# A chunked state recurrence with a shorter way back, two more kinds of copies and sums on the vector engine, and weight splits that no longer alternate between two engines

## The chip, the cores and the metric

The kernel runs on one core of one Trainium2 chip. The metric is device time in microseconds (us) of one execution. The engines are named as the profile names them: PE is the matrix engine, PEld its weight loads, DVE the vector engine, ACT the scalar engine, POOL the general engine (GpSimd), SP the engine that issues most DMAs.

## The reference

A network of two blocks over 256 context and 256 latent tokens. The change touches one layer of it, an S5 mixer: 128 groups of 16 channels, each with 64 complex states and two directions, that run over time by a linear recurrence in chunks. Cut to what matters for the change:

```python
def s5_scan(u, abar, bbar, cmat, h0):
...
        bu = jnp.einsum('btgn,gpn->btgp', u_blk.astype(jnp.complex64), bbar)
        bu = bu.at[:, 0].add(abar[None] * h)
...
        _, hs = lax.associative_scan(_linrec_combine, (a, bu), axis=1)
        y = jnp.einsum('btgp,gnp->btgn', hs, cmat).real
...
# s5_mixer, for each direction: the context first, then the latents from its last state
        yc_dir, h_ctx = s5_scan(flip_seq(uc, rev), abar, bbar, cmat, h0)
        y_dir, _ = s5_scan(flip_seq(u, rev), abar, bbar, cmat, h_ctx)
        y = y + flip_seq(y_dir, rev)
...
        g = jax.nn.gelu(t.reshape(bsz, n, E_WIDTH))
        return (g * jax.nn.sigmoid(g @ w + bias)).astype(p.dtype)
```

In words: each state is the decay times the state before plus an input term, s_t = a s_(t-1) + B u_t. The kernel needs y for the latents only; from the context it needs the last state.

## The kernel before, in words

The mixer runs over 512 tokens cut into 64 chunks of 8 steps (32 of the context and 32 of the latents). It works in four quarters q0 to q3 of 32 groups. For each quarter there are stages, each a Python generator in `s5_mix`:

- u: the input product for 512 channels in four units of weights (PE lines L200 to L202), then four evacuations from PSUM (the accumulator memory) by ACT into tiles of the ring Q.
- t: PE transposes of these tiles (L998), evacuated by ACT (L149, `h<-pm`, 128x512).
- x: eight passes of chunk sums (PE L1017), each evacuated by ACT into `Sc` (context) and `S` (latents); after the eighth, `recur` does the recurrence on DVE and makes `hy`, eight copies of S for PE.
- y: what the states give and what the inputs give in the same chunk (PE L1100 and L1077), then a gelu on ACT and DVE. y needs `hy` of its own quarter.
- z: the gate's product in four units, each evacuated by ACT as a tanh and a copy into one Q tile; the gate is then formed from both halves.
- g: the product of gelu and gate, which is the input of the GLU.

The stages are traced in one hand-written order:

```python
STAGES = "u0 z0/1 t0 z0/1 x0 u1 z0/1 t1 z0/1 x1 u2 z1/1 t2 y0 x2 w0 z1/1 u3 t3 y1 x3 w1 z1/2 z2 y2 w2 z3 y3 g0 g1 g2 w3 g3"
```

(z0/1 is one of the four units of z0; w is the last step of a y.) A scheduler then orders the instructions of each engine; every engine runs its own list in order. Tiles are taken from rings: a new tile of a ring takes the place of the one that was allocated so many tiles before, and its first writer waits until that one's last reader is done. The ring Q (`qslot`, 128x512) has 9 places and serves u, z, gelu and the temporaries `t1`, `t2` of `recur`; staged weights `st` have 6 places, split weights `wl` 3, PSUM tiles `pm` 4 and `pa` 3. The small temporaries `rt` of the serial part of `recur` have two places of their own.

Every weight unit (`wunit`) is loaded by SP into `st`, copied by ACT into its rounded half (`hi`, L149 `wl<-st` 128x1024), and the remainder (`lo = st - hi`, L152 `wl<-st,wl`) is formed by DVE or POOL as the pattern `lo_pat` says, letter by letter ("V" is DVE, "P" is POOL).

`recur` works in two parts. The first goes up over the 32 context chunks: five levels of sums, each of two products and two sums (a complex multiplication by a power of the decay from `ap`, a table loaded for each quarter), 24 instructions of up to 128x512 elements. The second goes through the 32 latent chunks one after the other: 31 times two products and two sums of 128x64.

Of the kernel before, what the change touches and what calls it, by code (L numbers as in the profile page):

```python
# [5 lines left out]
F32 = mybir.dt.float32  # L6
# [3 lines left out]
AF = mybir.ActivationFunctionType  # L10
ALU = mybir.AluOpType
# [94 lines left out]
def bc(ap, *dims):  # L106

    return bass.AP(tensor=ap.tensor, offset=ap.offset, ap=[list(ap.ap[0])] + [list(d) for d in dims])


class Builder:
# [850 lines left out]
    def s5_mix(self, hT, W):  # L962

        nc = self.nc
# [38 lines left out]
        def x_quarter(q):  # L1003
            ut = uts[q]
            Sc = self.S5.tile([128, 2, 32, 32], F32, tag="Sc", name="Sc", bufs=1)
            S = self.S5.tile([128, 2, 33, 32], F32, tag="S", name="S", bufs=2)
            for i in range(8):
                w = self.ST.tile([128, 1024], F32, tag="st", name="st")[:, :].rearrange("p (o x) -> p o x", o=4)
                self.dma(w, self.wd[:, 32 * q:32 * q + 32, :, :].rearrange("p (o i) d x -> p i o (d x)", i=8)[:, i])
                ps = self.pms()  # L1010
                for o in range(4):
                    g = 8 * o + i
                    x = ut[g // 16][:, g % 16, :]
                    xb = bass.AP(tensor=x.tensor, offset=x.offset + 31, ap=[list(x.ap[0]), [32, 2], [-1, 32]])
                    for r in range(2):
                        for d in range(2):
                            nc.tensor.matmul(ps[64 * d:64 * d + 64, r * 256 + o * 64:r * 256 + (o + 1) * 64],  # L1017
                                             w[:, o, d * 128 + r * 64:d * 128 + r * 64 + 64],
                                             x if d == 0 else xb, start=True, stop=True, tile_position=(0, 64 * d))
                pv = ps[:, :].rearrange("p (r o c) -> p r o c", r=2, o=4)  # L1020
                self.copy_a(Sc[:, :, :, i::8].rearrange("p r c o -> p r o c"), pv[:, :, :, :32])
                self.copy_a(S[:, :, 1:, i::8].rearrange("p r c o -> p r o c"), pv[:, :, :, 32:])
                if i == 7:
                    recur(q, Sc, S)
                yield

        def recur(q, Sc, S):
            ap = self.S5.tile([128, 5, 3, 32], F32, tag="ap", name="ap")
            self.dma(ap[:, :, :, :].rearrange("p a b g -> p (a b) g"),
                     self.apd[:, :, :, 32 * q:32 * q + 32].rearrange("p a b g -> p (a b) g"))  # L1030

            for k in range(5):
                st = 2 << k
                n = min(16 >> k, 8)
                for s0 in range((1 << k) - 1, 32, st * n):
                    t1, t2 = (self.qslot()[:, :64 * n].rearrange("p (r c g) -> p r c g", r=2, c=n) for _ in range(2))
                    x = bc(Sc[:, 0, s0, 0:1], (1024, 2), (32 * st, n), (1, 32))
                    xs = Sc[:, 1, s0, 0:1]
                    xs = bass.AP(tensor=xs.tensor, offset=xs.offset, ap=[list(xs.ap[0]), [-1024, 2], [32 * st, n], [1, 32]])
                    z = bc(Sc[:, 0, s0 + (1 << k), 0:1], (1024, 2), (32 * st, n), (1, 32))  # L1040
                    self.mul(t1, x, bc(ap[:, k, 0, 0:1], (0, 2), (0, n), (1, 32)))
                    self.mul(t2, xs, bc(ap[:, k, 1, 0:1], (32, 2), (0, n), (1, 32)))
                    self.add(t1, t1, z)
                    self.add(bc(S[:, 0, 0, 0:1], (1056, 2), (32, 1), (1, 32)) if k == 4 else z, t1, t2)
            are, aim = bc(ap[:, 0, 0, :], (0, 2), (1, 32)), ap[:, 0, 1:3, :]
            for c in range(1, 32):
                t = self.S5.tile([128, 2, 2, 32], F32, tag="rt", name="rt", bufs=2)
                old = S[:, :, c - 1, :]
                sw = bass.AP(tensor=old.tensor, offset=old.offset + 1056, ap=[list(old.ap[0]), [-1056, 2], [1, 32]])
                self.mul(t[:, 0], old, are)  # L1050
                self.mul(t[:, 1], sw, aim)
                self.add(S[:, :, c, :], S[:, :, c, :], t[:, 0])
                self.add(S[:, :, c, :], S[:, :, c, :], t[:, 1])
            hy = hys[q]
            hy += [self.S5.tile([128, 2, 16, 32], F32, tag="hy", name="hy", bufs=4) for _ in range(2)]
            for a in range(2):
                for r in range(2):
                    sc = 1.0 if r == 0 else -1.0
                    f = S[0:64, r, 0:32, a * 16:(a + 1) * 16].rearrange("p c g -> p g c")
                    b = S[64:128, r, 31, a * 16:a * 16 + 1]  # L1060
                    b = bass.AP(tensor=b.tensor, offset=b.offset, ap=[list(b.ap[0]), [1, 16], [-32, 32]])
                    nc.scalar.activation(hy[a][0:64, r, :, :], f, AF.Copy, scale=sc)
                    nc.scalar.activation(hy[a][64:128, r, :, :], b, AF.Copy, scale=sc)

        def y_quarter(q):
            ut, hy = uts[q], hys[q]
# [57 lines left out]
        def z_quarter(q):  # L1124
            if q < 2:
                zt = self.hslot()
            elif q == 2:
                zs.append(self.S5.tile([128, 2048], F32, tag="Sc", name="zs"))
            zt = (zt if q < 2 else zs[0][:, 1024 * (q - 2):1024 * (q - 1)])[:, :].rearrange("p (o x) -> p o x", o=4)
            for o in range(4):  # L1130
                ps = self.pacc()
                w = self.w_ws(W, 2048 + q * 512 + o * 128)
                for kt in range(8):
                    xs = [hT[kt][:, r, :].rearrange("p (s c) -> p s c", s=8)[:, :, 32:] for r in range(2)]
                    self.mm3(ps[:, :256].rearrange("p (s c) -> p s c", s=8), w[kt], xs, kt == 0, kt == 7)
                th = self.qslot()
                nc.scalar.activation(th[:, :256], ps[:, :256], AF.Tanh, scale=0.5)
                self.copy_a(th[:, 256:], ps[:, :256])
                self.mul(zt[:, o, :], th[:, :256], th[:, 256:], nc.gpsimd)
                self.add(zt[:, o, :], zt[:, o, :], th[:, 256:], nc.gpsimd)  # L1140
                if o == 3:
                    Z[q] = zt
                yield
# [19 lines left out]
        for stage in STAGES.split():  # L1163
            gs = []
            for p in stage.split("+"):
                p, _, n = p.partition("/")
                name = p.replace("w", "y")
                if name not in open_:
                    f, steps = gen[name[0]]
                    open_[name] = f(int(name[1])), steps  # L1170
                g, steps = open_[name]
# [807 lines left out]
    def build(self):  # L1979
        tc = self.tc  # L1980
        with tc.tile_pool(name="C", bufs=1) as self.C, \
                tc.tile_pool(name="H", bufs=16) as self.H, \
                tc.tile_pool(name="Q", bufs=9) as self.Q, \
                tc.tile_pool(name="T", bufs=8) as self.T, \
                tc.tile_pool(name="ST", bufs=NST) as self.ST, \
                tc.tile_pool(name="WL", bufs=NHI) as self.WL, \
                tc.tile_pool(name="DR", bufs=1, space=DRAM) as self.DR, \
                tc.tile_pool(name="PA", bufs=NPA, space=PSUM) as self.PA, \
                tc.tile_pool(name="PM", bufs=NPM, space=PSUM) as self.PM, \
                tc.tile_pool(name="PF", bufs=1, space=PSUM) as self.PF:  # L1990
            self.setup()
            with tc.tile_pool(name="SB", bufs=1) as self.SB, tc.tile_pool(name="E", bufs=NE) as self.E:
                self.extra = NE
                self.block1_l0()
                if "x1n" in self.dbg:
                    for b in range(4):
                        self.dma(self.dbg["x1n"][b * 128:(b + 1) * 128, :], self.x1[b])
                self.block2_vectors()
            self.lo_pat = "VP"
            self.off = tc.nc.gpsimd  # L2000
            self.extra = 0
            with tc.tile_pool(name="S5", bufs=1) as self.S5:
                G = self.block1_l1()
            with tc.tile_pool(name="X", bufs=1) as self.X, tc.tile_pool(name="E2", bufs=12) as self.E:
                self.extra = 8
                self.block2(self.block1_glu(G))
# [27 lines left out]
```

## Time and profile before

| | |
|---|---|
| median of 3 runs | 2326.35 us (2323.8 to 2330.18) |
| profiled execution, its own time | 2329.09 us |
| span in the profile | 2327.2 us (1.89 us lie outside it) |
| granted TensorE clock, mean | 0.909 of full |
| PE / DVE busy | 2030.9 us (87%) / 1429.4 us (61%) |
| ACT / POOL busy | 875.5 us (38%) / 749.3 us (32%) |
| DMA, mean | 158 GB/s |

PE is the engine that is busy most. The S5 layer lies between about 690 and 1130 us of the span. A busy share over the whole span says little of the stage that the change touches; for that one reads the windows, the waits and the timelines of that stretch.

### The profile page before, as it was taken

The page shows a single profiled execution, that of the slowest core. Times are in us where ns is not written, and L with a number is a line of the kernel's source. Part 1 is how long each engine was busy: PE and PEld are TensorE (multiplying, and loading weights), DVE is VectorE, ACT ScalarE, POOL GpSimd, SP SyncE. Part 2 cuts the span into 40 slices and gives each one's busy share as a digit, 9 for nine tenths or more (in the row PEclk, how much of TensorE's full clock was granted, in tenths as well). Part 3 has the DMA queues.
Part 4 walks back from the last instruction along what each step waited for, and adds up shares of the span by engine and source line. Part 5 has one row for each costly group of instructions (what it writes and reads, how often), then busy time and mean ns, then how long its engine had stood idle before and what let it go on. Part 6 is the DMA issues. An engine that isn't in the chain of part 4 may idle for free. (4 is left out here: it accounts for less than half of the span.)

```text
span 2327.2 us, 34638 instructions
## 1 busy us (share of the span) xinstructions
PE 2030.9 (87%) x13236; PEld 1597.8 (69%) x13236; DVE 1429.4 (61%) x2945; ACT 875.5 (38%) x1650; POOL 749.3 (32%) x501
## 2 busy tenths in 40 slices
PE   5697788999987878659888899999999999988998
PEld 3575565677766676547786565778888877657997
DVE  5788887766695867564547735553333466455556
ACT  2234233334434453534434243343222244334443
POOL 1687877800013201323333210122111513112334
PEclk9897877999998987879999979999999999889999
DMA  7656535544554576989465606433333226354663
GB/s 265 181 181 204 182 110 162 154 164 140 187 165 117 184 182 168 233 193 289 145 231 161 189 15 234 138 91 91 105 95 93 89 75 184 133 175 134 191 190 118
DMA packets 362775, 368.56 MB, mean 158 GB/s; under 512 B 27512, under 2 KB 291420, under 8 KB 362608
## 3 DMA queue, kind: packets, MB, share of 16 engines
q1 hardware_dynamic: 356048, 355.32, 50.9%
q0 software_dynamic: 2208, 6.29, 0.9%
q10 hardware_dynamic: 4352, 4.72, 0.6%
q8 instruction: 105, 1.72, 0.3%
q14 instruction: 62, 0.51, 0.1%
HBM read 319.62 MB, written 46.65 MB: 157 GB/s over the span
## 5 line engine op out<-in xcount | busy, mean ns | idle before, releaser
L149 ACT ACTIVATE wl<-st 128x1024 fp32r<-128x1024 f32 (+1 forms) x332 | 344.4, 1043 | 491.7 <-PE pa L202 165.7
L152 POOL TENSOR_TENSOR wl<-st,wl 128x1024 fp32r<-128x1024 f32 (+1 forms) x98 | 237.3, 2422 | 873.9 <-ACT wl L149 846.8
L152 DVE TENSOR_TENSOR wl<-st,wl 128x1024 fp32r<-128x1024 f32 (+1 forms) x234 | 321.3, 1376 | 269.2 <-ACT wl L149 268.4
L200 PE MATMUL pa<-h,wl 128*128 128x512 f32 (+1 forms) x1152 | 403.5, 353 | 10.5 <-DVE q L158 6.4
L202 PE MATMUL pa<-h,wl 128*128 128x512 f32 (+1 forms) x1152 | 401.6, 350 | 8.0 <-DVE wl L152 7.6
L201 PE MATMUL pa<-h,wl 128*128 128x512 f32 (+1 forms) x1152 | 402.9, 351 | 0.0
L200 PEld LDWEIGHTS pa<-h,wl 128*128 128x128 f32 x1152 | 220.3, 192 | 46.4 <-issue 7.9
L202 PEld LDWEIGHTS pa<-h,wl 128*128 128x128 f32 x1152 | 220.5, 192 | 38.7 <-DVE wl L152 8.7
L201 PEld LDWEIGHTS pa<-h,wl 128*128 128x128 f32 x1152 | 220.8, 192 | 27.8 <-issue 0.2
L201 PE MATMUL pa<-wl,h 128*128 128x512 f32 (+1 forms) x560 | 224.5, 404 | 16.8 <-DVE wl L152 15.3
L200 PE MATMUL pa<-wl,h 128*128 128x512 f32 (+1 forms) x560 | 218.9, 407 | 18.6 <-ACT wl L149 7.4
L202 PE MATMUL pa<-wl,h 128*128 128x512 f32 (+1 forms) x560 | 215.3, 400 | 9.8 <-DVE h L152 5.7
L152 POOL TENSOR_TENSOR h<-q,h 128x256 fp32r<-128x256 f32 (+2 forms) x82 | 95.3, 1170 | 213.4 <-ACT h L149 137.1
L168 DVE SCALAR_TENSOR_TENSOR q<-q,pa 128x512 f32<-128x512 f32 (+1 forms) x104 | 58.9, 567 | 166.7 <-ACT q L1861 91.7
L149 ACT ACTIVATE h<-pm 128x512 f32<-128x512 f32 (+3 forms) x182 | 93.0, 545 | 170.0 <-PE pm L1529 46.4
L201 PE MATMUL pm<-wl,h 128*128 128x512 f32 (+1 forms) x376 | 146.6, 393 | 2.7 <-DVE wl L152 2.0
L200 PEld LDWEIGHTS pa<-wl,h 128*128 128x128 f32 x560 | 110.2, 199 | 55.0 <-ACT h L149 11.4
L202 PE MATMUL pm<-wl,h 128*128 128x512 f32 (+1 forms) x376 | 143.2, 393 | 0.0
L201 PEld LDWEIGHTS pa<-wl,h 128*128 128x128 f32 x560 | 111.7, 199 | 45.3 <-DVE wl L152 18.1
L299 PE MATMUL pf<-st,cs 128*32 128x512 f32 x576 | 98.2, 688 | 50.8 <-DMA st<-in_w_ada_dram 25.0
L200 PE MATMUL pm<-wl,h 128*128 128x512 f32 (+1 forms) x376 | 139.6, 391 | 1.0 <-ACT wl L149 1.0
L202 PEld LDWEIGHTS pa<-wl,h 128*128 128x128 f32 x560 | 109.8, 198 | 35.7 <-DVE h L152 7.2
(352 smaller groups left out, 3768.4 us busy)
## 6 DMA issues: line engine op xcount, KB each, us to landing
st<-in_w_ada_dram SPq DMA_DIRECT2D x96, 512.0 KB, 5.3
st<-in_ada_w_dram SPq DMA_DIRECT2D x48, 512.0 KB, 5.7
st<-in_w_ffn_gate_dram SPq DMA_DIRECT2D x44, 512.0 KB, 4.2
st<-in_w_ffn_up_dram SPq DMA_DIRECT2D x44, 512.0 KB, 3.9
st<-in_w_ffn_down_dram SPq DMA_DIRECT2D x44, 512.0 KB, 3.7
st<-in_attn_w_in_dram SPq DMA_DIRECT2D x40, 512.0 KB, 4.8
st<-in_w_out_dram SPq DMA_DIRECT2D x40, 512.0 KB, 4.0
wd<-w SPq DMA_DIRECT2D x64, 256.0 KB, 4.3
```

The source lines that it names most:

```text
L149: self.nc.scalar.activation(o, i, AF.Copy)
L152: (eng or self.nc.vector).tensor_tensor(o, a, b, op=ALU.subtract)
L168: self.nc.vector.scalar_tensor_tensor(o, a, s, b, op0=op0, op1=op1)
L200: mm(o, w[0], x[0], start=start, stop=False)
L201: mm(o, w[0], x[1], start=False, stop=False)
L202: mm(o, w[1], x[0], start=False, stop=stop)
L299: mm = nc.tensor.matmul(ps[32 * q:32 * q + 32, :], self.cs[:, blk, kt, :, :], st[:, (q % 2) * 512:(q % 2 + 1) * 512], start=k0 == 0, stop= ...
```

## The change

1. In `recur` a function `step` does one complex multiply and add for up to eight chunks at once. The way up uses it with the same instructions as before. The 31 serial steps are replaced: sums of pairs (16 chunks, two groups of four instructions), sums of fours (8 chunks, one group), then seven single chunks one after the other, then back to the pairs (7 chunks, one group) and to the rest (15 chunks, two groups). These are 52 instructions instead of 124. Their temporaries come from the ring Q, two for each group of four; before, the second part used `rt`.
2. Of the eight `hy` copies of a quarter four go to DVE; four, with the scale -1, stay on ACT.
3. The gate in z is one DVE instruction, (tanh + 1) * p, instead of a product and a sum on POOL.
4. `lo_pat` of this layer is "V" instead of "VP": all remainders are formed by DVE.

```diff
+            def step(T, rs, z0, x0, st, n, k, out=None):
+                for j in range(0, n, 8):
+                    m = min(8, n - j)
+                    z0j, x0j = z0 + st * j, x0 + st * j
+                    t1, t2 = (self.qslot()[:, :64 * m].rearrange("p (r c g) -> p r c g", r=2, c=m) for _ in range(2))
...
+                    self.mul(t1, x, bc(ap[:, k, 0, 0:1], (0, 2), (0, m), (1, 32)))
+                    self.mul(t2, xs, bc(ap[:, k, 1, 0:1], (32, 2), (0, m), (1, 32)))
+                    self.add(t1, t1, z)
+                    self.add(z if out is None else out, t1, t2)
             for k in range(5):
-                st = 2 << k
-                n = min(16 >> k, 8)
...
-            are, aim = bc(ap[:, 0, 0, :], (0, 2), (1, 32)), ap[:, 0, 1:3, :]
-            for c in range(1, 32):
-                t = self.S5.tile([128, 2, 2, 32], F32, tag="rt", name="rt", bufs=2)
...
-                self.mul(t[:, 0], old, are)
-                self.mul(t[:, 1], sw, aim)
-                self.add(S[:, :, c, :], S[:, :, c, :], t[:, 0])
-                self.add(S[:, :, c, :], S[:, :, c, :], t[:, 1])
+                step(Sc, 1024, (2 << k) - 1, (1 << k) - 1, 2 << k, 16 >> k, k,
+                     bc(S[:, 0, 0, 0:1], (1056, 2), (32, 1), (1, 32)) if k == 4 else None)
+            step(S, 1056, 1, 0, 2, 16, 0)
+            step(S, 1056, 3, 1, 4, 8, 1)
+            for c in range(7, 32, 4):
+                step(S, 1056, c, c - 4, 1, 1, 2)
+            step(S, 1056, 5, 3, 4, 7, 1)
+            step(S, 1056, 2, 1, 2, 15, 0)
...
-                    nc.scalar.activation(hy[a][0:64, r, :, :], f, AF.Copy, scale=sc)
-                    nc.scalar.activation(hy[a][64:128, r, :, :], b, AF.Copy, scale=sc)
+                    for p0, i in ((0, f), (64, b)):
+                        if r == 0:
+                            nc.vector.tensor_copy(hy[a][p0:p0 + 64, r, :, :], i)
+                        else:
+                            nc.scalar.activation(hy[a][p0:p0 + 64, r, :, :], i, AF.Copy, scale=-1.0)
...
-                self.mul(zt[:, o, :], th[:, :256], th[:, 256:], nc.gpsimd)
-                self.add(zt[:, o, :], zt[:, o, :], th[:, 256:], nc.gpsimd)
+                self.stt(zt[:, o, :], th[:, :256], 1.0, th[:, 256:], ALU.add, ALU.mult)
...
-            self.lo_pat = "VP"
+            self.lo_pat = "V"
```

How the lists of the engines change is seen at three places. In the names, `h<-pm` is a transposed tile of the t stage, `q<-pm` with 128x8x16 an evacuation of u, `hy<-S` a copy of the states.

The first place is ACT's list after u1, before x1. In the kernel before it reads (the copies `hy` of q0 stand some 30 rows further down):

```order
L149 ACTIVATE q_6539<-pm_6411 128x8x16
L1137 ACTIVATE q_6578<-pa_6548 128x256
L149 ACTIVATE q_6578<-pa_6548 128x256
L149 ACTIVATE h_6583<-pm_6584 128x512
L149 ACTIVATE h_6583<-pm_6602 128x512
L149 ACTIVATE h_6620<-pm_6621 128x512
L149 ACTIVATE h_6620<-pm_6639 128x512
```

and in the changed kernel:

```order
L149 ACTIVATE q_6460<-pm_6332 128x8x16
L149 ACTIVATE h_6503<-pm_6504 128x512
L1068 ACTIVATE hy_6319<-S_6034 64x512 x2
L1068 ACTIVATE hy_6320<-S_6034 64x512 x2
L1142 ACTIVATE q_6499<-pa_6469 128x256
L149 ACTIVATE q_6499<-pa_6469 128x256
L149 ACTIVATE h_6503<-pm_6522 128x512
L149 ACTIVATE h_6540<-pm_6541 128x512
L149 ACTIVATE h_6540<-pm_6559 128x512
```

The four `hy` copies of q0 now stand ahead of one z evacuation and of three of the four transposed tiles that x1 reads.

The second place is DVE's list at the end of q2's recurrence, in the changed kernel (L165, the lines L158 with `pm`, and L168 are the gelu of y1; `wl_7743` is the remainder of the fourth weight unit of u3):

```order
L155 TENSOR_TENSOR q_7548<-q_7548,S_7275 128x512
L165 TENSOR_SCALAR q_7598<-q_7598 128x512
L165 TENSOR_SCALAR q_7607<-q_7607 128x512
L168 SCALAR_TENSOR_TENSOR h_7047<-q_7646 128x256
L155 TENSOR_TENSOR q_7554<-q_7554,S_7275 128x448
L155 TENSOR_TENSOR S_7275<-q_7548,q_7549 128x2x8x32
L158 TENSOR_TENSOR q_7598<-q_7598,pm_7587 128x512
L158 TENSOR_TENSOR q_7607<-q_7607,pm_7588 128x512
L155 TENSOR_TENSOR S_7275<-q_7554,q_7555 128x2x7x32
L152 TENSOR_TENSOR wl_7743<-st_7741,wl_7743 128x1024
```

and the same remainder in the kernel before, in POOL's list:

```order
L152 TENSOR_TENSOR wl_7980<-st_7978,wl_7980 128x1024
```

It has moved from an engine of its own to a place behind the last instruction of q2's recurrence.

The third place is the end of q3's recurrence on DVE in the changed kernel (`zs` is the gate of q2 and q3, the `wl` behind it are the four weight units of z3):

```order
L155 TENSOR_TENSOR S_7983<-q_8262,q_8263 128x2x7x32
L168 SCALAR_TENSOR_TENSOR h_8305<-q_8306,pm_8295 128x128 x4
L1066 COPY hy_8268<-S_7983 64x512 x2
L1066 COPY hy_8269<-S_7983 64x512 x2
L168 SCALAR_TENSOR_TENSOR zs_8392<-q_8457 128x256
L152 TENSOR_TENSOR wl_8696<-st_8694,wl_8696 128x1024
...
L152 TENSOR_TENSOR wl_8730<-st_8728,wl_8730 128x1024
...
L152 TENSOR_TENSOR wl_8764<-st_8762,wl_8764 128x1024
...
L152 TENSOR_TENSOR wl_8798<-st_8796,wl_8798 128x1024
```

Half of the `hy` copies and all four remainders of z3 now stand behind the recurrence on the same engine.

## Rows read from the trace of the kernel before

**Rows 1.** One window: start:end, us, busy per engine (instructions), granted clock, DMA share, GB/s

```profile
1000.00:1025.00 25.00, 7.66 (x55) 6.20 (x54) 18.29 (x82) 9.86 (x15) 4.33 (x6) 0.64 0.85 156
```

**Rows 2.** PE's waits, 690 to 1130 us: us in total, times, longest

```profile
PE pm L1100 <- ACT hy L1063: 18.4, 4, 16.0
...
PE pm L1017 <- DMA st<-wd: 11.8, 10, 2.6
...
PE pm L371 <- DVE h L165: 7.6, 1, 7.6
PE pm L1100 <- DMA st<-vd: 6.5, 5, 2.4
```

**Rows 3.** Lines by form, 690 to 1130 us: busy us, mean ns, idle before

```profile
L1062 ACT ACTIVATE hy<-S 64x512 f32<-64x512 f32 x16 | 17.6, 1099 | 20.7 <-DVE S L155 20.5
...
L149 ACT ACTIVATE h<-pm 128x512 f32<-128x512 f32 x20 | 11.8, 596 | 22.5 <-PE pm L1077 18.2 <-PE pm L998 4.3
```

**Rows 4.** Timeline of DVE, recurrences of q0 and q1: start, us, [idle before, releaser]

```profile
768.13 4.68 DVE L158 TENSOR_TENSOR q<-Sc,ap 128x512 f32<-128x512 f32 x4
...
819.75 2.50 DVE L158 TENSOR_TENSOR q<-Sc,ap 128x512 f32<-128x512 f32 x4 [4.01 <-DMA ap<-apd]
822.16 1.29 DVE L155 TENSOR_TENSOR q<-q,Sc 128x512 f32<-128x512 f32 x2
...
827.28 2.58 DVE L152 TENSOR_TENSOR wl<-st,wl 128x1024 fp32r<-128x1024 f32 x1 [1.23 <-ACT wl L149]
...
834.66 0.36 DVE L158 TENSOR_TENSOR rt<-S,ap 128x64 f32<-128x64 f32 x2
...
835.45 0.36 DVE L158 TENSOR_TENSOR rt<-S,ap 128x64 f32<-128x64 f32 x2
```

**Rows 5.** Timeline of DVE and POOL around a remainder, recurrence of q3

```profile
985.76 3.05 DVE L155 TENSOR_TENSOR S<-S,rt 128x64 f32<-128x64 f32 x2
986.39 2.34 POOL L152 TENSOR_TENSOR wl<-st,wl 128x1024 fp32r<-128x1024 f32 x1
...
989.26 1.22 DVE L152 TENSOR_TENSOR wl<-st,wl 128x1024 fp32r<-128x1024 f32 x1
```

**Rows 6.** Timeline of DVE and ACT, q2's recurrence and y0's gelu

```profile
891.38 0.69 DVE L155 TENSOR_TENSOR Sc<-q 128x512 f32<-128x512 f32 x1
...
892.10 0.60 ACT L1113 ACTIVATE q<-pm 128x512 f32<-128x512 f32 x1 [5.79 <-DVE Sc L155]
```

**Rows 7.** Timeline from x1 to u2, all engines

```profile
793.78 6.75 PE L1017 MATMUL pm<-h,st 128*64 128x64 f32 x224
796.84 4.10 SPq L146 DMA_DIRECT2D st<-in_s_w_in_dram  x5
...
802.90 1.06 ACT L149 ACTIVATE wl<-st 128x1024 fp32r<-128x1024 f32 x1 [3.00 <-DMA st<-in_s_w_in_dram]
...
807.88 0.67 ACT L149 ACTIVATE S<-pm 128x256 f32<-128x256 f32 x1
...
812.68 0.80 PE L201 MATMUL pa<-wl,h 128*128 128x512 f32 x1 [7.48 <-DVE wl L152]
```

**Rows 8.** Timeline of PE: y0, the end of x2, u3

```profile
842.06 2.90 PE L1100 MATMUL pm<-st,hy 128*32 128x128 f32 x96
...
871.68 1.98 PE L1017 MATMUL pm<-h,st 128*64 128x64 f32 x32 [1.51 <-DMA st<-wd]
...
905.60 0.80 PE L201 MATMUL pa<-wl,h 128*128 128x512 f32 x1 [1.34 <-POOL wl L152]
```

**Rows 9.** Timeline of DVE, ACT and PE: recurrence of q3, its copies, the GLU

```profile
955.99 2.50 DVE L158 TENSOR_TENSOR q<-Sc,ap 128x512 f32<-128x512 f32 x4 [0.20 <-ACT Sc L149]
...
1017.46 0.48 DVE L155 TENSOR_TENSOR S<-S,rt 128x64 f32<-128x64 f32 x2
...
1025.62 1.06 ACT L1063 ACTIVATE hy<-S 64x512 f32<-64x512 f32 x1
...
1046.63 0.56 PE L200 MATMUL pm<-h,wl 128*128 128x256 f32 x1
```

More of the change, by code (lines that the diff above doesn't have):

```diff
@@ L1030, in recur @@
                      self.apd[:, :, :, 32 * q:32 * q + 32].rearrange("p a b g -> p (a b) g"))
-            for k in range(5):
-                st = 2 << k
-                n = min(16 >> k, 8)
[L1035 to L1044, printed above, removed]
@@ L1045, in recur @@
-            are, aim = bc(ap[:, 0, 0, :], (0, 2), (1, 32)), ap[:, 0, 1:3, :]
-            for c in range(1, 32):
-                t = self.S5.tile([128, 2, 2, 32], F32, tag="rt", name="rt", bufs=2)
-                old = S[:, :, c - 1, :]
-                sw = bass.AP(tensor=old.tensor, offset=old.offset + 1056, ap=[list(old.ap[0]), [-1056, 2], [1, 32]])
-                self.mul(t[:, 0], old, are)
-                self.mul(t[:, 1], sw, aim)
-                self.add(S[:, :, c, :], S[:, :, c, :], t[:, 0])
-                self.add(S[:, :, c, :], S[:, :, c, :], t[:, 1])
+            def step(T, rs, z0, x0, st, n, k, out=None):
[3 more added lines that the diff above has]
+                    t1, t2 = (self.qslot()[:, :64 * m].rearrange("p (r c g) -> p r c g", r=2, c=m) for _ in range(2))
+                    x = bc(T[:, 0, x0j, 0:1], (rs, 2), (32 * st, m), (1, 32))
+                    xs = T[:, 1, x0j, 0:1]
+                    xs = bass.AP(tensor=xs.tensor, offset=xs.offset, ap=[list(xs.ap[0]), [-rs, 2], [32 * st, m], [1, 32]])
+                    z = bc(T[:, 0, z0j, 0:1], (rs, 2), (32 * st, m), (1, 32))
+                    self.mul(t1, x, bc(ap[:, k, 0, 0:1], (0, 2), (0, m), (1, 32)))
+                    self.mul(t2, xs, bc(ap[:, k, 1, 0:1], (32, 2), (0, m), (1, 32)))
+                    self.add(t1, t1, z)
+                    self.add(z if out is None else out, t1, t2)
@@ L1057, in recur @@
                 for r in range(2):
-                    sc = 1.0 if r == 0 else -1.0
                     f = S[0:64, r, 0:32, a * 16:(a + 1) * 16].rearrange("p c g -> p g c")
```

## The prediction, made before the changed kernel ran

> **What bounds it now.** PE is busy 87% of the span, so first I ask where it isn't. In the window 1000 to 1025 us it works 7.66 of 25 us at a granted clock of 0.64, while DVE works 18.29 [rows 1]: in the S5 layer it is a chain that limits, not PE. The table of PE's waits for that layer then says for what PE waits: 18.4 us for `hy` (one wait of 16.0), 11.8 and 6.5 us for the tables `wd` and `vd` from DRAM, and 7.6 us for a sum of the norm ahead of the layer [rows 2]. `hy` itself waits 20.5 us for DVE's S [rows 3]. So the recurrence of a quarter sets PE's time only where PE needs its `hy` at once, which is plainly so in q3 [rows 2]; in q0 to q2 PE has another quarter's u, t and x meanwhile. The timeline of DVE then gives prices [rows 4], and those of the stages give the handovers [rows 7 to 9].
>
> **Prices of the recurrence.** The way up of q1 runs from 819.75 to 834.66: 14.91 us, less one remainder of 2.58 and a gap of 1.23, leaves 11.1 us. One serial chunk is 835.45 - 834.66 = 0.79 us, 31 of them 24.5 us [rows 4]. For the new way I use the same rows: two products and two sums of 128x512 take 2.50/2 + 1.29 = 2.5 us; a group of 448 elements about 2.3. Pairs 2 x 2.5, fours 2.5 + 0.3 for its dependent ends, seven single chunks 7 x 0.79 = 5.5, back 2.3, the rest 2.5 + 2.3: in all 20.4, say 20.5 us. The 72 instructions less save only **4.0 us per quarter**, since the remaining ones are wide. All four quarters together would be 16 us if each lay on the path.
>
> **The remainders.** Sixteen of the 32 move from POOL to DVE. On POOL one takes 2.34 us; DVE's own takes 1.22 [rows 5]. While POOL's ran, two sums of DVE that take 0.79 - 0.36 = 0.43 us of an undisturbed chunk [rows 4] took 3.05 [rows 5]: 2.6 us of DVE lost for one POOL remainder, against 1.2 if DVE does it itself, so 1.4 us gained for each of the four that fall into q3's recurrence. The Trainium skill, Perfetto Trace Analysis, section Optimizing Scalar/DVE Operations, says that moving work between these two engines might not help, since they share a read port of SBUF. By that rule the move gains nothing, and the sum would come out some 5 us higher, at 2346. The trace bears out that the two hinder each other, but not that the exchange is even, so I go by the row.
>
> **The ring Q, which decides.** The new way takes its t1 and t2 from Q: 13 groups, 26 tiles, so that a quarter's recurrence takes 38 tiles of Q and not 12. The ring has 9 places. That a new tile waits for the one nine before it is seen in the trace: ACT's square of y0's gelu began at 892.10, when DVE's sum that had begun at 891.38 and taken 0.69 was done, after a wait of 5.79 us [rows 6]; that sum is the last reader of the tile nine places back. Before, the U tiles of the next quarter fell behind tiles from the middle of the way up. Now the nine tiles ahead of U0 are those of the last four groups and more: the four U tiles take the places of t2 of chunk 27, t1 and t2 of chunk 31 and t1 of the seven pairs, and z's tile that of their t2. So **u's evacuation of the next quarter, and with it t and x, waits until the recurrence of this quarter is nearly done**; before, it ran beside it. ACT's list makes it worse: the four `hy` copies, which wait for the last S, stand ahead of the transposed tiles that x needs (first place of the change).
>
> Step by step, in the time of the profiled execution:
>
> - q0: the recurrence starts at 768.1 [rows 4]. With 11.1, three remainders of DVE (3.7) and 20.5, S is done at 803.4. Four `hy` on ACT at 1.1 [rows 3] make 807.8; one z evacuation and three transposed tiles at 0.6 [rows 3] make 810.2. x1 starts there, against 793.78 [rows 7]: +16.4.
> - x1: its last evacuation of S ended 14.8 us after its start (807.88 + 0.67, rows 7), so q1's recurrence starts at 825.0; before it was 819.75, held by the table `ap` [rows 4], whose load is now issued early enough. So of 16.4 only 5.3 remain. u2's weights, issued 3.1 us into x1 and landing 6.1 later [rows 7], give u2 its remainder at about 821.6 (812.68 before); u2 isn't the bound.
> - q1: 825.0 + 11.1 + 2.4 (two remainders) + 20.5 = 859.0; `hy` 4.4 and the first transposed tiles 1.2: y0 and x2 start near 864.7, against 842.06 [rows 8]: +22.6. The big loss: before, u2's evacuation and t2 were hidden beside this recurrence.
> - y0 and x2 go at the pace of DMAs into the six `st` places, 31.6 us from 842.06 to the end at 873.66 [rows 8]: x2 ends at 896.3, its evacuation 1.3 later at 897.6.
> - q2: the fourth remainder of u3 stands on DVE behind the last S (second place of the change). 897.6 + 11.1 + 4.9 (four remainders) + 1.2 (a wait for a rounded half, like the 1.23 in rows 4) + 20.5 + 2.6 (four gelu instructions) + 1.2 = 939.1, where u3 went on at 905.60 [rows 8]: **+33.5**.
> - y1 and x3 follow u3 at the same distance, so q3's recurrence starts near 955.99 + 33.5 = 989.5 [rows 9].
> - q3, the gain: before, its S ended 1017.94 - 955.99 = 62 us after its start and the last `hy` 70.7 us after it [rows 9], stretched by POOL's remainders and gate, gelu and DVE's own remainders. Now 11.1 + 3.7 + 20.5 + 3.3 (five gelu instructions) = 38.6 to the last S, four `hy` on ACT (4.4) and what stands between (2.6): 45.6 us, **25.1 less**. The other four `hy` run on DVE beside ACT's. z3's four remainders now stand behind them on DVE, with y3 in between: 4.9 is given back. Net gain **20.2**.
> - One remainder more stands on DVE ahead of the norm that PE waits for at the layer's start [rows 2]: **+1.2**.
>
> Sum: +33.5 - 20.2 + 1.2 = **+14.5**. The profiled execution took 2329.09 us, so the changed kernel's would be 2343.6; it lay 2.74 above the median of its runs, so I predict 2340.9, **2341 us** (+0.6%).
>
> Unknown prices. DVE's `hy` copy of 64x512 doesn't occur before: between the 0.69 of a 128x512 sum [rows 6] less something for half the partitions, so perhaps 0.35, and ACT's 1.10 [rows 3]; I take 0.6, and even 1.1 lies beside ACT's four (4.4). The gate in one instruction of 128x256: between 0.35 and 0.69, sixteen times 5.6 to 11 us of DVE, mostly beside z's products; four of them stand in q3's stretch, within +-0.7 of what I took. What the clock does is not in the sum: after the 7.48 us wait PE's first product took 0.80 us [rows 7], and the new idle stretches before x1 and y0 are longer. 2 to 4 us more, at most, for a few slow products after each.
>
> **The rivals.**
>
> - *A, faster: the evacuations aren't held.* If the tiles' places come free early (or ACT's list still overlaps), the loss doesn't occur, and what remains is what the parts save: PE's wait of 16.0 for `hy` [rows 2] and of 7.48 for a remainder [rows 7], 23.5 us together: 2303. For it: u before ran hidden. Against it: the wait of rows 6, exactly on the ring. It decides if u2's evacuation starts before q1's seventh single chunk. By the same section of the Trainium skill DVE pays some 60 ns for each instruction and larger operations pay where the engine is saturated: an estimate of 4 x 72 x 0.06 = 17 us, so 2309 if all of it were on the path. My row of 0.79 us for four small instructions, about 0.2 each, agrees that small ones are dear, but DVE's length is on the path alone in q3.
> - *B, no change: DMA absorbs the delay.* PE waits 11.8 + 6.5 = 18.3 us for `wd` and `vd` [rows 2]; if these tables load while PE stands, x2 and y0 make up for it: 2341 - 18.3 = 2323. Against it: six places of `st`, which are full after the first idle us.
> - *C, slower still: q3 gives nothing back.* If y3 is bound by z3, whose remainders and evacuations are now in line behind the `hy` copies, only the recurrence's own 4.0 are kept of the 20.2: 2357. From y3's start more than 60 us after q3's start on it decides.
>
> **How the numbers follow.** A change of 0.3% (7 us) is about what a measurement of this kernel can tell from none. My own case 0.58, own range 2331 to 2351; six parts of 58 of it below 2333.3 count as same. A 0.16 (one part of it within 0.3%), B 0.14 (11 parts same, 3 just beyond to either side), C 0.12. Slower: 0.52 + 0.02 + 0.12 = 0.66; same 0.06 + 0.11 + 0.01 = 0.18; faster 0.15 + 0.01 = 0.16. The range leaves out most of A and reaches over B, my case and C: 2320 to 2359; bounds of the unknown costs lie within.
>
> **What the new profile would show.** If I am right: ACT's evacuations of u1 and u2 wait for DVE with gaps that end with the chunks 27 to 31 of the recurrence; PE stands idle before x1 and again before y0, for 15 us and more; no group of `rt`, and a recurrence of 31 to 36 us from its first product to its last S in all quarters; u3's fourth unit waits for DVE `wl`; the wait for `hy` in y3 starts earlier and is far shorter than 16 us. If u's tiles are evacuated while the way up still runs, the main step is wrong and A holds; if x2's and y0's waits for DMA vanish, B; if the GLU starts more than 80 us after q3's recurrence, C.

## The result, and the profile after

The changed kernel took 2338.77 us in the median of five runs (2334.69 to 2343.78), the kernel before 2325.41 in five beside it: ratio 1.0064, interval 1.0049 to 1.0078. Forecast were 2341 us and +0.6%.

The profiled execution is the shortest of the five, and it reached the layer 2.6 us earlier than the one of before, for reasons outside the change. So I measure the layer by itself: from PE's first product behind the norm (L371) to the first of L322 in the GLU, a place that every kernel here has. Timeline of PE before, start and duration in us:

```profile
702.76 1.54 PE L371 MATMUL pm<-cst,h 128*128 128x128 f32 x6 [7.58 <-DVE h L165]
...
1103.21 0.60 PE L322 MATMUL pf<-cst,q 128*128 128x128 f32 x4
```

That is 400.4 us. In the changed kernel the same two rows (the first and the last of its timelines below) are 413.1 us apart, **12.7 us more**. The head of its page:

```profile
span 2332.9 us, 34329 instructions
...
PE 2028.8 (87%) x13236; PEld 1598.9 (69%) x13236; DVE 1425.9 (61%) x2705; ACT 859.1 (37%) x1634; POOL 685.0 (29%) x453
```

DVE has 240 instructions less, ACT and POOL are 16 and 64 us less busy, and the kernel is slower: busy time says nothing here. PE's waits between 690 and 1130 us, the view of [rows 2] (us in total, times, longest):

```profile
PE pm L998 <- ACT q L149: 20.2, 5, 9.7
PE pm L1017 <- DMA st<-wd: 19.5, 12, 2.8
PE pm L1105 <- DMA st<-vd: 17.3, 8, 5.4
PE pa L200 <- ACT q L149: 16.6, 2, 11.4
PE pm L371 <- DVE h L165: 7.8, 1, 7.8
```

The wait for `hy` is gone from the top [rows 2]. In its place t (L998) waits 20.2 us for u's evacuations, and z's products (L200) wait 16.6 us for z's evacuations, which come late on ACT. The copies by form, the view of [rows 3]:

```profile
L1068 ACT ACTIVATE hy<-S 64x512 f32<-64x512 f32 x16 | 18.0, 1123 | 5.9 <-DVE S L155 5.8
...
L1066 DVE COPY hy<-S 64x512 f32<-64x512 f32 x16 | 10.0, 628 | 0.3
```

The DVE copy takes 0.63 us (forecast: 0.6). The timeline of DVE, ACT and PE shows the hold in q0:

```profile
700.20 1.12 PE L371 MATMUL pm<-cst,h 128*128 128x128 f32 x4 [7.82 <-DVE h L165]
...
762.31 2.49 DVE L158 TENSOR_TENSOR q<-Sc,ap 128x512 f32<-128x512 f32 x4
...
775.36 2.50 DVE L158 TENSOR_TENSOR q<-S,ap 128x512 f32<-128x512 f32 x4
...
788.56 0.23 DVE L155 TENSOR_TENSOR S<-q 128x64 f32<-128x64 f32 x1
...
788.88 0.61 ACT L149 ACTIVATE q<-pa 128x128 f32<-128x128 f32 x3 [13.18 <-DVE S L155]
...
789.72 1.97 PE L998 MATMUL pm<-cst,q 64*64 64x64 f32 x32 [9.68 <-ACT q L149]
...
790.84 0.76 DVE L155 TENSOR_TENSOR S<-q 128x64 f32<-128x64 f32 x2
...
791.10 0.61 ACT L149 ACTIVATE q<-pa 128x128 f32<-128x128 f32 x3 [1.43 <-DVE S L155]
...
796.36 4.47 ACT L1068 ACTIVATE hy<-S 64x512 f32<-64x512 f32 x4 [2.63 <-DVE S L155]
...
801.38 1.59 ACT L149 ACTIVATE h<-pm 128x512 f32<-128x512 f32 x3
...
803.58 2.61 PE L1017 MATMUL pm<-h,st 128*64 128x64 f32 x82
```

PE had finished u1 at 780.0. ACT stood 13.18 us and began 0.09 us after the sum of chunk 27 ended (788.56 + 0.23); the second tile began at 791.10, when the first of the two sums of 790.84, that of chunk 31, was done. That is the place of U0 and U1 in the ring as it was worked out. The later steps, on the same view:

```profile
818.93 0.69 DVE L158 TENSOR_TENSOR q<-Sc,ap 128x512 f32<-128x512 f32 x1
...
857.56 4.45 PE L1105 MATMUL pm<-st,hy 128*32 128x128 f32 x96 [1.88 <-ACT h L149]
...
886.84 1.98 PE L1017 MATMUL pm<-h,st 128*64 128x64 f32 x32 [1.04 <-DMA st<-wd]
...
889.50 2.50 DVE L158 TENSOR_TENSOR q<-Sc,ap 128x512 f32<-128x512 f32 x4 [31.95 <-ACT Sc L149]
...
919.93 0.60 ACT L1118 ACTIVATE q<-pm 128x512 f32<-128x512 f32 x1 [18.39 <-DVE S L155]
...
922.70 0.38 ACT L1142 ACTIVATE q<-pa 128x256 f32<-128x256 f32 x1
...
923.40 0.80 PE L200 MATMUL pa<-wl,h 128*128 128x512 f32 x1 [11.36 <-ACT q L149]
...
929.50 1.22 DVE L152 TENSOR_TENSOR wl<-st,wl 128x1024 fp32r<-128x1024 f32 x1
...
930.77 0.50 PE L201 MATMUL pa<-wl,h 128*128 128x512 f32 x1 [0.44 <-DVE wl L152]
...
977.90 2.50 DVE L158 TENSOR_TENSOR q<-Sc,ap 128x512 f32<-128x512 f32 x4 [0.20 <-ACT Sc L149]
...
1014.20 0.63 DVE L155 TENSOR_TENSOR S<-q 128x448 f32<-128x448 f32 x1
...
1017.21 4.51 ACT L1068 ACTIVATE hy<-S 64x512 f32<-64x512 f32 x4
...
1024.89 1.03 PE L1105 MATMUL pm<-st,hy 128*32 128x128 f32 x6 [5.01 <-DMA st<-vd]
...
1050.55 0.39 PE L200 MATMUL pm<-h,wl 128*128 128x256 f32 x1 [0.70 <-ACT wl L149]
...
1113.33 0.60 PE L322 MATMUL pf<-cst,q 128*128 128x128 f32 x4
```

At 923.40 PE waits for z's evacuation, but what is held there is a tile of the gelu. ACT stands 18.39 us at a square of y0's gelu (L1118), whose new Q tile takes a place of chunk 27 (the sum of that chunk ends at 919.90). z's evacuation (L1142) stands behind the two squares in ACT's list and starts as soon as they are done. The wait of 5.3 us before z's product at 1007.97 has the same form, with a square of y1's gelu that waited 15.81 us.

### The profile page after: what moved, and what is told of

It reads as the page before. It is cut to its first block, busy times and chain, and to the rows that moved or that the text cites. A ratio compares the mean times of both kernels' runs of the same rounds, so it can differ in the third digit from the quotient of the medians.

```text
span 2332.9 us, 34329 instructions
## 1 busy us (share of the span) xinstructions
PE 2028.8 (87%) x13236; PEld 1598.9 (69%) x13236; DVE 1425.9 (61%) x2705; ACT 859.1 (37%) x1634; POOL 685.0 (29%) x453
## 5 line engine op out<-in xcount | busy, mean ns | idle before, releaser
L152 DVE TENSOR_TENSOR wl<-st,wl 128x1024 fp32r<-128x1024 f32 (+1 forms) x250 | 341.5, 1370 | 250.3 <-ACT wl L149 249.6
L200 PE MATMUL pa<-h,wl 128*128 128x512 f32 (+1 forms) x1152 | 406.6, 355 | 13.7 <-DVE q L158 6.4
L152 POOL TENSOR_TENSOR wl<-st,wl 128x1024 fp32r<-128x1024 f32 (+1 forms) x82 | 199.0, 2427 | 695.2 <-ACT wl L149 667.6
L200 PEld LDWEIGHTS pa<-h,wl 128*128 128x128 f32 x1152 | 223.1, 195 | 49.3 <-issue 7.9
L202 PEld LDWEIGHTS pa<-h,wl 128*128 128x128 f32 x1152 | 223.1, 194 | 31.4 <-DVE wl L152 1.7
L201 PEld LDWEIGHTS pa<-h,wl 128*128 128x128 f32 x1152 | 223.8, 194 | 27.6 <-issue 0.2
L200 PE MATMUL pa<-wl,h 128*128 128x512 f32 (+1 forms) x560 | 218.1, 405 | 26.1 <-ACT q L149 11.4
L168 DVE SCALAR_TENSOR_TENSOR q<-q,pa 128x512 f32<-128x512 f32 (+1 forms) x104 | 59.0, 567 | 166.8 <-ACT q L1865 91.6
L200 PEld LDWEIGHTS pa<-wl,h 128*128 128x128 f32 x560 | 109.2, 197 | 61.3 <-ACT q L149 11.8
L200 PE MATMUL pm<-wl,h 128*128 128x512 f32 (+1 forms) x376 | 139.3, 391 | 1.0 <-ACT wl L149 1.0
L201 PEld LDWEIGHTS pa<-wl,h 128*128 128x128 f32 x560 | 110.3, 197 | 36.5 <-DVE wl L152 11.8
```

Of the source, the lines that this page charges most:

```text
L152: (eng or self.nc.vector).tensor_tensor(o, a, b, op=ALU.subtract)
L168: self.nc.vector.scalar_tensor_tensor(o, a, s, b, op0=op0, op1=op1)
L200: mm(o, w[0], x[0], start=start, stop=False)
L201: mm(o, w[0], x[1], start=False, stop=False)
L202: mm(o, w[1], x[0], start=False, stop=stop)
```

## The experiments

My theory: the 26 tiles of Q that the way back takes hold up the evacuations of u and z, and through them t, x and y; the parts 2 to 4 gain. The rivals: the loss comes from the places of copies and remainders in the lists of ACT and DVE, or from the number of Q tiles. Each run is timed beside the kernel before; "layer" is the time from L371 to L322 of its own profile.

| | median us | ratio to before | interval | layer us |
|---|---|---|---|---|
| before | 2325.41 | 1 | | 400.4 |
| changed | 2338.77 | 1.0064 | 1.0049 to 1.0078 | 413.1 |
| e1 temporaries in hy | 2307.19 | 0.9931 | 0.9916 to 0.9946 | 385.8 |
| e2 recurrence alone | 2363.95 | 1.0167 | 1.0143 to 1.0191 | 433.8 |
| e3 old recurrence, parts 2 to 4 | 2306.54 | 0.9934 | 0.9915 to 0.9954 | 385.1 |
| e4 remainders alone | 2319.23 | 0.9979 | 0.9960 to 0.9998 | 391.7 |
| e5 first six tiles in Q | 2308.34 | 0.9948 | 0.9929 to 0.9968 | 388.3 |
| e6 last six tiles in Q | 2337.57 | 1.0067 | 1.0042 to 1.0091 | 413.6 |
| e7 all hy on DVE | 2342.86 | 1.0081 | 1.0051 to 1.0110 | 420.5 |
| e8 no tile of the recurrence in Q | 2311.33 | 0.9947 | 0.9929 to 0.9965 | 386.9 |
| e9 e1 with remainders VP | 2312.05 | 0.9959 | 0.9940 to 0.9979 | 391.0 |
| e10 e1 with the gate on POOL | 2304.26 | 0.9919 | 0.9898 to 0.9939 | 385.2 |
| e11 e2 with temporaries in hy | 2329.00 | 1.0022 | 1.0003 to 1.0040 | 401.6 |
| e12 hy copies alone | 2317.36 | 0.9973 | 0.9958 to 0.9987 | 394.1 |

The layer is that of one execution and not a median: the profiled executions of e2, e4 and e11 lay 14, 10 and 16 us below the median of their kernel. Differences of a few us between layers are to be read beside the ratios.

**e1_own_temps.** The hy tiles of a quarter are written only after its recurrence, so they can carry its temporaries: no memory more, nothing else changed in the code.

```diff
-   t1, t2 = (self.qslot()[:, :64 * m]... for _ in range(2))
+   h = hy[next(alt)][:, :, :, :].rearrange("p r a b -> p r (a b)")
+   tt = [self.qslot() if T is Sc else h[:, i, :] for i in range(2)]
+   t1, t2 = (t[:, :64 * m]... for t in tt)
```

> The changed kernel, but the temporaries of the new way back are taken from the hy tiles of the same quarter (not yet written then), not from the ring Q; same instructions, same sizes. Theory (ring): u1's and u2's evacuations no longer wait for the end of the recurrence, x1 starts before 796 us, y0 before 848, u3's last unit before 908, and with the gain of q3 kept (about 15 us) the median comes to 2303 to 2314, faster than before. Rival (the copies' and remainders' places in the lists of ACT and DVE hold things up): it stays at 2333 to 2343.

2307.19 us, ratio 0.9931: from 0.6% slower to 0.7% faster by the place of the temporaries, 27.3 us in the layer (413.1 - 385.8). In its timeline ACT takes u1 from PSUM while the way back still runs, and waits for PE only:

```profile
787.34 2.15 ACT L149 ACTIVATE q<-pa 128x128 f32<-128x128 f32 x12 [2.33 <-PE pa L202]
```

In its waits of PE, L998 stands 0.4 us behind `q` and L200 not at all. The four longest:

```profile
PE pm L1017 <- ACT S L149: 18.0, 3, 11.2
PE pm L1017 <- DMA st<-wd: 16.8, 9, 3.9
PE pm L1108 <- DVE hy L1069: 12.5, 1, 12.5
PE pm L1108 <- DMA st<-vd: 11.2, 7, 5.9
```

Of the starts that I wrote down x1's was missed (799.11, not before 796), since this execution reached the layer 4.4 us later than before's (L371 at 707.16). y0 (843.1) and u3's last unit (904.85) came in time. That the gain of q3 is kept did not come true: q3's recurrence took 58.3 us here, in the changed kernel 36.9 (see the end of the next section).

**e2_rec_only.** The kernel before with the new recurrence, Q and all; parts 2 to 4 undone.

```diff
-            for c in range(1, 32):   # serial, tiles rt
...
+            step(S, 1056, 1, 0, 2, 16, 0)   # and the rest of the new way back, tiles of Q
```

> The kernel before with the new recurrence alone (temporaries in Q); remainders VP, hy on ACT, gate on POOL as before. Theory (ring): the loss up to u3 stays (about 25 us) and the gain of q3 shrinks to a few us of the recurrence: 2338 to 2352, slower than the changed kernel or equal. Rival (the loss comes with the parts that moved work to DVE): 2312 to 2326.

2363.95 us: slower still, and 12 us beyond what I had written. The rival is out: without the parts that moved work the loss is larger. Its waits of PE:

```profile
PE pm L998 <- ACT q L149: 32.0, 5, 12.5
...
PE pa L200 <- ACT q L149: 16.8, 2, 11.2
...
PE pm L1103 <- ACT h L149: 6.5, 1, 6.5
```

t waits 32.0 us for u's evacuations where it was 20.2. What stands on the held path (eight copies on ACT, remainders on POOL) now costs in each quarter, while before it cost in q3 only; that is how I read it, and I did not take the two apart here.

**e3_old_serial.** The changed kernel with the 31 serial chunks and `rt`.

```diff
-            step(S, 1056, 1, 0, 2, 16, 0)   # and the rest of the way back
+            for c in range(1, 32):
+                t = self.S5.tile([128, 2, 2, 32], F32, tag="rt", name="rt", bufs=2)
```

> The changed kernel with the old recurrence (31 serial chunks, rt tiles), so the remainders, the hy copies and the gate alone. Theory (ring): no hold, x1 before 798 us, only the gain of q3: 2306 to 2320. Rival (these parts make the loss): 2333 or more.

2306.54 us: as fast as e1. Parts 2 to 4 gain 15.3 us in the layer, and the new recurrence adds nothing to them here even without its hold.

**e4_lo_only** and **e12_hy_split_only.** One part each in the kernel before.

```diff
-            self.lo_pat = "VP"
+            self.lo_pat = "V"
```

> The kernel before with lo_pat V alone: all remainders of the layer on DVE. Theory, by the price of a disturbed pair of sums (2.6 us lost to one POOL remainder against 1.2 of DVE's own): 4 to 12 us less, 2314 to 2322. Rival (the exchange between the two engines is even): 2324 to 2329.

2319.23 us, 8.7 us in the layer, by the ratio 4.9 us (0.5 to 9.3); the interval ends just below 1. So the exchange is not quite even: the price taken from [rows 5] has the right sign.

```diff
+                    for p0, i in ((0, f), (64, b)):
+                        if r == 0:
+                            nc.vector.tensor_copy(hy[a][p0:p0 + 64, r, :, :], i)
+                        else:
+                            nc.scalar.activation(hy[a][p0:p0 + 64, r, :, :], i, AF.Copy, scale=-1.0)
```

> The kernel before with part 2 alone: four of the eight hy copies of a quarter on DVE, four on ACT. e9_own_temps_vp (without the remainders) kept 0.4% and e11_rec_only_own (without remainders, copies and gate) lost 0.2%, so copies and gate together should bring about 0.6%, and e10_own_temps_zpool gives the gate nothing. Theory (the copies, 4.4 us a quarter, bring it): 2308 to 2318. Rival (parts 1 to 4 don't add up; the copies alone are worth their 4.4 us of q3 at most): 2317 to 2325.

2317.36 us, 6.3 us in the layer, on the border of the two. With e4's 8.7 it makes 15.0 of the 15.3 of e3; by the ratios it is 4.9 + 6.3 = 11.2 of 15.3, which the intervals allow too. So the two parts make up most of e3, and little is left for the gate.

**e5_first_six_in_q** and **e6_last_six_in_q.** Both take six more tiles of Q a quarter than before; only which groups take them differs. The edits are shown against e1.

```diff
-   tt = [self.qslot() if T is Sc else h[:, i, :] ...]
+   tt = [self.qslot() if T is Sc or n in (16, 8) else h[:, i, :] ...]   # e5
+   tt = [self.qslot() if T is Sc or n in (7, 15) else h[:, i, :] ...]   # e6
```

> As e1_own_temps, but the first three groups of the way back (pairs, fours: six tiles) take their temporaries from Q, the rest from hy. Theory (ring, and in it the place alone): the four tiles of u follow on tiles whose last reader is the end of the way up or the first pairs, free before PE has finished the next u, so no hold: 2303 to 2313 as e1_own_temps. Rival (it is the number of Q tiles, 18 a quarter instead of 12): between, 2312 to 2325.

> As e1_own_temps, but the last three groups of the way back (7 and 15 chunks: six tiles) take their temporaries from Q, the rest from hy. Same number of Q tiles as e5_first_six_in_q. Theory (ring): the fourth tile of u waits for the last groups as in the changed kernel, so it is slow like that one: 2328 to 2345. Rival (the number of tiles): equal to e5_first_six_in_q within 4 us.

2308.34 against 2337.57 us: e5 is as fast as e1, e6 as slow as the changed kernel. It isn't the number of tiles, it is how late the tile nine places back is read for the last time. In e6 three of u1's four tiles go out at once and the fourth waits, in the timeline of ACT and DVE:

```profile
779.80 0.67 ACT L149 ACTIVATE q<-pa 128x128 f32<-128x128 f32 x3
780.27 0.36 ACT L149 ACTIVATE q<-pm 128x128 f32<-128x128 f32 x1
...
791.02 0.62 DVE L155 TENSOR_TENSOR S<-q 128x448 f32<-128x448 f32 x1
...
791.67 0.45 ACT L149 ACTIVATE q<-pa 128x128 f32<-128x128 f32 x2 [11.04 <-DVE S L155]
```

Its tile lies nine places behind the first temporary of the seven pairs, whose last reader ends at 791.02 + 0.62 = 791.64. One tile out of four held for 11 us is enough: PE's next product, one of z (L200), waits 11.2 us for this evacuation, and t comes behind it. In PE's waits:

```profile
PE pa L200 <- ACT q L149: 20.3, 3, 11.2
```

**e7_hy_all_dve.** The changed kernel with no copy on ACT.

```diff
-                            nc.scalar.activation(hy[a][p0:p0 + 64, r, :, :], i, AF.Copy, scale=-1.0)
+                            self.ts(hy[a][p0:p0 + 64, r, :, :], i, -1.0, ALU.mult)
```

> The changed kernel with all eight hy copies on DVE (the scale -1 as a product with a constant), so that none stands in ACT's list ahead of the transposed tiles. The prediction's term of 4.4 us per quarter for ACT's hy at x1 and y0 says 4 to 9 us less than the changed kernel: 2329 to 2335. Rival (ACT's copies lie beside DVE's, the tiles wait for PE anyway): 2336 to 2343.

2342.86 us: no gain, the intervals of it and of the changed kernel overlap. x1 started 106.4 us after L371, in the changed kernel 103.4. That ACT's copies stand ahead of the transposed tiles is not a cause of the loss that can be had back this way. This matters for e1 and e5 too: the scheduler orders every kernel anew, and there ACT's copies of q0 come behind the first passes of x1, in e6 and in the changed kernel ahead of the transposed tiles. By e7 that order alone is not what made e1 and e5 fast.

**e8_all_temps_hy.** e1 with the way up in hy as well.

```diff
-   tt = [self.qslot() if T is Sc else h[:, i, :] for i in range(2)]
+   tt = [h[:, i, :] for i in range(2)]
```

> As e1_own_temps, and the way up takes its temporaries from hy too, so that the recurrence has no tile in Q. Theory: u, z and gelu wait for no recurrence at all; the gelu's wait of 5 us in q2 goes too: 2295 to 2306, the fastest so far. Rival (nothing of it lies on the path): 2306 to 2312.

2311.33 us: the number of the rival, but not its reason. q3's recurrence started 234.8 us after L371, in e1 245.6, so something did lie on the path up to there. The 10.8 us were lost in q3: its recurrence took 71.0 us (58.3 in e1), in which DVE stood 17.6 us for ACT, and y3 waited for it. In PE's waits:

```profile
PE pm L1108 <- DVE hy L1069: 14.4, 1, 14.4
```

**e9_own_temps_vp** and **e10_own_temps_zpool.** e1 without part 4, and e1 without part 3.

```diff
-            self.lo_pat = "V"
+            self.lo_pat = "VP"                                               # e9
...
-   self.stt(zt[:, o, :], th[:, :256], 1.0, th[:, 256:], ALU.add, ALU.mult)
+   self.mul(zt[:, o, :], th[:, :256], th[:, 256:], nc.gpsimd)               # e10
+   self.add(zt[:, o, :], zt[:, o, :], th[:, 256:], nc.gpsimd)
```

> e1_own_temps with lo_pat VP, so that every second remainder goes to POOL again. Without the ring's hold, what are the remainders on DVE worth? Prediction's price (2.6 us lost to a POOL remainder, 1.2 for DVE's own, four in q3 on the path, others in q0 to q2 partly): 5 to 15 us more than e1_own_temps, 2312 to 2322. Rival (even exchange): 2304 to 2311.

> e1_own_temps with the gate of z as a product and a sum on POOL, as in the kernel before. The prediction put the gate at nothing (0.35 to 0.69 us of DVE a piece, beside z's products): 2305 to 2311. Rival (POOL's two small instructions hold DVE up as its remainders do): 2311 to 2318.

e9: 2312.05 us, 5.2 us more in the layer than e1, at the lower end of what was expected. e10: 2304.26 us, 0.6 us in the layer: the gate is worth nothing, as forecast; it is the fastest of all by its median, but its interval overlaps those of e1 and e3.

**e11_rec_only_own.** e2 with e1's edit.

> The kernel before with the new recurrence alone, its way back with temporaries in hy: part 1 of the change without the ring's hold; beside e2_rec_only this prices the hold without the other parts. Prediction's 4.0 us per quarter, on the path in q3 alone, and less of POOL's disturbance since the stretch is shorter: 2312 to 2322. Rival (the shorter recurrence is worth nothing): 2322 to 2328.

2329.00 us, 1.2 us more in the layer than before: both expectations missed on the side of "worth nothing". Beside e2 it gives the hold alone, without parts 2 to 4: 433.8 - 401.6 = 32.2 us, by the ratios 33.7.

## Why the prediction was right

By its own steps, shifts of the changed kernel's profile against before's [rows 7 to 9], with 2.6 us added for its earlier start of the layer (700.20 against 702.76):

| step | forecast | measured |
|---|---|---|
| x1 starts | +16.4 | 803.58 - 793.78 + 2.6 = +12.4 |
| q1's recurrence starts | +5.3 | 818.93 - 819.75 + 2.6 = +1.8 |
| y0 and x2 start | +22.6 | 857.56 - 842.06 + 2.6 = +18.1 |
| y0 and x2 last | 31.6 | 886.84 + 1.98 - 857.56 = 31.3 |
| u3 goes on | +33.5 | 930.77 - 905.60 + 2.6 = +27.8 |
| q3's recurrence starts | +33.5 | 977.90 - 955.99 + 2.6 = +24.5 |
| q3, start to last S / last hy | 38.6 / 45.6 | 36.9 / 43.8 |
| gain from q3's start to the GLU | 20.2 | 24.5 - 12.7 = 11.8 |
| the norm's wait | +1.2 | 7.82 - 7.58 = +0.2 |
| sum | +14.5 | +12.7 |

- **The ring** was the right step, and e1, e5 and e6 show it: place in the ring and not number of tiles; e7 speaks against the order of the copies. It was sized about 6 us too high up to u3. I took q0's start of 768.1 as given [rows 4]; it came 5.8 us sooner, at 762.31, and only 2.6 of that are the earlier layer. The first four products there then took 2.49 us, before 4.68. The way back itself took 796.28 - 775.36 less one remainder of 1.2, 19.7 us for 20.5.
- **The remainder behind q2's last S** came as said: it began at 929.50, and u3's products followed at 930.77. (The gelu in that list is y0's and not y1's, whose products start only at 940.52.) But on the same path PE had been held for 11.36 us up to 923.40, by the square of y0's gelu that waits on the ring ahead of z's evacuation. The wait of that square was in [rows 6], 5.79 us before; I had used it as proof of the ring and left it out of the sum, where it grew to 18.39.
- **q3's gain** is the term that was off: 11.8 for 20.2. The recurrence and the copies were as short as forecast, but y3 didn't profit: after the last `hy` the GLU's first product came 28.8 us later (1050.55 - 1021.72) where it had been 20.0 [rows 9], and I had allowed 4.9 for that. Another 6.2 us were lost in the GLU's first products: 62.8 us from there to L322 (1113.33 - 1050.55), before 56.6. y3 now waits 5.01 us for one `vd` alone, and the waits for `vd` in the layer rose from 6.5 [rows 2] to 17.3. It is a piece of rival C that I gave to C alone; C itself did not come, since y3 started 47.0 us after q3's recurrence (C: more than 60) and the GLU 72.7 us after it (C: more than 80). Whether the DMA or z3 in between sets the loss I did not separate.
- So errors of 9.0 us up to q3's start (5.7 of them up to u3) and 8.4 behind it, of opposite sign, and one of 1.0 nearly cancel. The 3.3 us between u3 and q3's start were to stay as before; x there waited less for ACT's evacuations (13.3 us in the layer before, now 3.3). The sign and the cause are shown; that the sum came within some 2 us of the median is partly luck.
- **The signs** came in part. The gaps of u1 and u2 end with the chunks 27 to 31, no `rt` is left, and u3 waits for DVE's `wl`. PE stood idle 9.7 us before t1 and 9.0 before t2, not 15 and more. From the first product to the last S it is 34.0 and 32.8 us in q0 and q1, 40.1 and 36.9 in q2 and q3: the 31 to 36 "in all quarters" did not even fit the prediction's own sums for these two (40.3 and 38.6). What I left to the clock is of the order allowed: PE was busy 313.7 us in the layer, before 308.2, at a mean granted clock of 0.84, before 0.85.
- **Rival A** was wrong here but near the value: with the hold gone (e1) the time is 2307, where A said 2303. Its reason was wrong: I gave 16.0 us to y3's wait for `hy` and 7.48 to a remainder as if all of both went away; in e1 y3 still waits 12.5 us for `hy`. e3 and e11 show that the shorter recurrence pays nothing in these lists, and that the copies (6.3 us, e12) and remainders (8.7 us, e4) pay. The estimate that I had made from the Trainium skill's cost per instruction (Perfetto Trace Analysis, Optimizing Scalar/DVE Operations) finds no support in e11: 288 DVE instructions less, layer +1.2 us.
- **Rival B** is out: x2 and y0 took 31.3 us (before 31.6) though PE stood idle for 9.0 us before t2, 12 us ahead of them; waits for `wd` even rose from 11.8 [rows 2] to 19.5.
- **The remainders' price** was 1.4 us for each of four in q3. e4 and e9 give 8.7 and 5.2 us in the layer for the sixteen, by the ratios 4.9 and 6.5 (e9's interval overlaps e1's), so the sign of the row holds. Its place does not: of e4's 8.7 us 7.5 fall ahead of q3's start (245.7 us after L371, before 253.2) and 1.2 behind it. A remainder is also done sooner on DVE, in 1.2 us and not 2.3 [rows 5]; no run tells the two causes apart. The Trainium skill (Perfetto Trace Analysis, Optimizing Scalar/DVE Operations) says that moving work between these two engines might not help; e4's ratio of 0.9979 (0.9960 to 0.9998) is a small gain.

What became of the 4.0 us of DVE per quarter shows in q3, the quarter that PE waits for. DVE's timeline there in e1:

```profile
952.83 2.50 DVE L158 TENSOR_TENSOR q<-Sc,ap 128x512 f32<-128x512 f32 x4 [0.21 <-ACT Sc L149]
...
977.99 0.43 DVE L168 SCALAR_TENSOR_TENSOR zs<-q 128x256 f32<-128x256 f32 x1 [3.12 <-ACT q L149]
...
990.43 1.23 DVE L152 TENSOR_TENSOR wl<-st,wl 128x1024 fp32r<-128x1024 f32 x1 [1.67 <-ACT wl L149]
...
1011.11 2.48 DVE L1069 COPY hy<-S 64x512 f32<-64x512 f32 x4
```

From the first product to the copies it is 58.3 us, hardly less than the 62.0 to the last S before; in e11 it is 60.3. The recurrence's own instructions take 29 us of DVE in e1 as in the changed kernel. But with the hold gone its list has seven remainders among them and not three, eight gates and not one, the gelu of two quarters and not of one, and DVE stands 8.1 us for ACT. So "worth nothing" is what the shorter recurrence is worth in these lists, in which it isn't shorter where PE waits for it. No run without the hold kept q3's recurrence together, so what it would be worth then stays open.

The second place is x2. In e1 two of its passes wait for ACT, whose list has a weight copy ahead of the evacuation:

```profile
875.32 1.06 ACT L149 ACTIVATE wl<-st 128x1024 fp32r<-128x1024 f32 x1 [12.54 <-DMA st<-in_s_w_in_dram]
...
877.65 0.61 ACT L149 ACTIVATE Sc<-pm 128x256 f32<-128x256 f32 x1
```

PE stands 11.2 us there, which e3 doesn't. In e11 the waits of x for ACT's evacuations come to 30.1 us, before to 13.3. It may be the order that the scheduler chose rather than the recurrence; no run undid it.

## What to carry to other kernels

A temporary from a shared ring can cost time although its own stage doesn't wait: count back from the *next* stages' tiles as many places as the ring has, and look when that old tile is read for the last time. A serial stage with many short tiles at its end makes the ring a barrier; its temporaries belong into a tile that is dead at that time (here the stage's own output). Look also at what stands behind a held instruction in its engine's list, as z's evacuation did behind the gelu. And count a shorter chain as a gain only after you have seen that the stage that waits for it gets it sooner: 72 instructions less per quarter were worth nothing in these lists, while two cheap moves (half of the copies and all remainders to DVE) brought 15 us.

## What the runs showed of the hardware

- A copy of 64x512 with strided reads took 0.63 us on DVE and 1.12 on ACT, both engines at once. ACT without DVE's copies beside it had taken 1.10 [rows 3], DVE without ACT's took 0.62 (e7): in this pairing neither slowed the other.
- Six more tiles of the ring per quarter cost nothing when the first groups of the way back take them (e5) and 29 us when the last groups do (e6), with the same instructions.
